# The RWKV stage of a decoder step: from one stream of head pairs with fillers to seven streams that hand over in DRAM

## The chip, the cores and the metric

The kernel runs on one core of a Trainium2 chip. Its time is the device time of one execution in microseconds; lower is better. The core has TensorE (matrix products, into eight PSUM banks), VectorE (DVE), ScalarE (ACT), GpSimd (POOL) and SyncE (SP, which here only issues DMAs). Each engine works through its own instructions in order and waits on semaphores for the others. A wait therefore also holds up whatever stands behind the waiting instruction on the same engine, and that goes for the DMAs in a queue too.

## The reference

One layer of a hybrid decoder is computed for 1024 prompt tokens and for eight sample sequences of eight tokens, 1088 columns in all, with a model width of 1024 and everything in fp32. The part that the change concerns is the RWKV-7 branch (8 heads of 64 channels) and what stands next to it:

```python
P = h @ w_in                                  # RWKV columns | pooling columns | gate columns
xl = pr + (pr_prev - pr) * mu_shift           # token shift
r, k, v, xw, xa, xg = split(xl)
decay = exp(-exp(-softplus(-(w0 + tanh(xw) @ w2)) - 0.5));  a = sigmoid(a0 + xa @ a2)
kk = normalize(k * k_k);  k = k * (1 + (a - 1) * k_a)
# per token and head, S is the 64x64 state:
sa = S @ (-kk);  S = S * decay + outer(sa, kk * a) + outer(v, k);  y = S @ r
y = group_norm(y) * ln_w + ln_b + sum(r * k * r_k) * v;  y = y * (sigmoid(xg) @ g2)
# branch B: causal means over 2, 4, 8, 16 tokens, minus the token, times pool_w
merged = sigmoid(gate_A) * (A @ w_br_rwkv) + sigmoid(gate_B) * (B @ w_br_pool)
x = x + gt * (merged @ w_out)                 # then a squared-ReLU MLP of width 4096, and norms
```

The recurrence over tokens is computed in chunks of 64 tokens: within a chunk its effect is a product with the inverse of a unit triangular 64x64 matrix, and only a 64x64 state goes from chunk to chunk. The prompt has 16 chunks; the 64 sample columns are one more, the 17th, in which eight 8x8 blocks are independent.

## The kernel before

Features lie on the 128 partitions, tokens along the free dimension. Two heads fill the partitions, so that the RWKV work comes in four blocks `f` of two heads.

**Weight jobs.** The large products are jobs in `stream` (line 177). A job takes weights of 128 outputs, splits weights and activations into a high and a low part of the fast fp32r type, and adds three products (`mm3`, line 169) for each of three column chunks `CH` (364, 362, 362 columns). The high part is made on ScalarE (line 165), the low one on GpSimd or VectorE (line 166). A job accumulates in three of four PSUM banks with the tag "mm"; its `consume` moves them out chunk by chunk.

**The order on TensorE is written out by the program.** `Pace.run` (line 87) keeps a clock of its own, to which every matmul adds a planned time. It takes the weight jobs as a background and a list of generators as foreground streams. A stream yields a due time (or a condition); as soon as the clock has reached it, its next step goes in ahead of the next piece of background. The order is fixed from then on: if a step's operands come later than planned, TensorE waits for them, with all that stands behind. The streams use two PSUM banks with the tag "w" and two with the tag "wc". The order on the other engines, SP included, is made by a scheduler.

**Stage 1** (`phase1`, line 1075) runs 34 jobs on `w_in`: 14 blocks of RWKV columns (`rwkv_cols`), 4 of pooling columns (`pool_cols`), 16 of gates (`gate`). Each collects its 1088 columns in a row (`px`, two buffers), finishes them (token shift, running sums, tanh) and stores them in DRAM (`d_x`, `d_th`). Then come eight jobs of the pooling branch (`op_job`), whose results stay in on-chip rows. The foreground streams are `chains`, `heads`, `pools` and `or_rows`. In `heads`, block after block:

- `front(f)`: decay, normalised key and rate over all 1088 columns; it makes `bk` (two operands of the score products, line 562 on VectorE and 563 on GpSimd) and leaves the rest for `unit`;
- `scores(f)`: `unit` for the two halves of the prompt and the sample chunk. It makes `ra` (lines 608 and 609), the score matmuls, masks (lines 628, 629) and transposes;
- `inverse(f)`: the triangular 16x16 blocks by a recursion of 15 steps on VectorE (lines 698, 700). Its tiles have two layers: the 16 prompt chunks, and the sample chunk with 15 empty places;
- `level` and `affine`: from 16x16 to 64x64 on TensorE, and the products that turn a chunk into one affine step;
- beside them, as a filler that `both` interleaves: `sample(f-1)` next to the front, `post(f-1)` (norm, bonus, output gate) next to the inverse.

`chains` (line 1025) carries the state through the 16 chunks: a product, an addition on VectorE (line 831), the next product, planned 2300 ns apart.

**Stage 2** (`phase2`, line 1158) begins with eight jobs of the RWKV branch (`or_job`, line 1176). Each loads a gate row into a tile "t" (four buffers), multiplies it with the product, adds the pooling result on GpSimd (line 1186), and splits the sum (lines 1189, 1190). The modulation weights (`ada`) take tiles of the same tag, two at a time. Then come `w_out`, the MLP and the final norm.

## Time and profile before

| | |
|---|---|
| median of 3 runs | 1866.54 us (1862.32 to 1871.72) |
| the profiled execution: time, span | 1863.12 us, 1861.3 us |
| mean granted TensorE clock | 0.963 |
| RWKV stage, from the first weight job to the last pooling-branch job | 84 to 858 us |
| branch, output and feed-forward jobs | 858 to 1861 us |

The profile shows one execution. Its page gives busy times of each engine, the same in 40 slices, the chain of work that ended last, and the costliest groups of instructions; other views give the waits of an engine, stretches of time, and single instructions. PE is TensorE, PEld its weight loads, PEclk the clock that it was granted, in parts of full speed. A row of the waits names who waited, for whom, the microseconds in all, the number of waits and the longest.

### The profile page before, as it was taken

The numbers are of one execution on the slowest core, as the hardware profiler recorded it, in microseconds if no ns is written. First come the engines' busy times: TensorE is split into PE (matmuls) and PEld (weight loads), VectorE is DVE, ScalarE is ACT, GpSimd is POOL, SyncE is SP. The second block draws the span as 40 slices with busy tenths as digits, with TensorE's granted clock in tenths as the row PEclk, the third lists the DMA queues.
The fourth block names the chain that finished last, engine by engine and source line by source line (L and its number), as shares of the span: only waits on it lengthen the run. The fifth ranks groups of instructions, "written<-read, shape, count | busy, mean of one in ns | idle before, by whom it ended". The sixth has DMA issues, their size and how long they took to land. (4 is left out here: it accounts for less than half of the span.)

```text
span 1861.3 us, 32532 instructions
## 1 busy us (share of the span) xinstructions
PE 1720.2 (92%) x13721; PEld 1597.2 (86%) x13721; DVE 867.1 (47%) x1446; ACT 557.6 (30%) x1085; POOL 421.9 (23%) x444
## 2 busy tenths in 40 slices
PE   3979997999798979998999789999999999999997
PEld 1869786887687779887889789999999999999987
DVE  5365647653765356444423653333333243433335
ACT  4533343343334324321223332222212121212132
POOL 2553234221312132011411431111111111111110
PEclk9989998999898989999999889999999999999999
DMA  8223322332232232445851211111111111111112
GB/s 313 68 85 117 123 68 78 119 99 77 81 114 99 74 107 81 167 142 205 286 184 66 74 57 41 46 46 46 43 44 46 46 46 46 40 46 46 46 46 97
DMA packets 76449, 169.96 MB, mean 91 GB/s; under 512 B 15152, under 2 KB 21808, under 8 KB 76304
## 3 DMA queue, kind: packets, MB, share of 16 engines
q1 hardware_dynamic: 70688, 151.68, 23.9%
q10 hardware_dynamic: 5472, 15.70, 2.5%
q8 instruction: 108, 1.77, 0.4%
q0 software_dynamic: 144, 0.51, 0.1%
q14 instruction: 37, 0.30, 0.1%
HBM read 133.47 MB, written 34.39 MB: 90 GB/s over the span
## 5 line engine op out<-in xcount | busy, mean ns | idle before, releaser
L147 PE MATMUL mm<-hx,whi 128*128 128x362 f32 (+1 forms) x2560 | 680.7, 348 | 9.9 <-DMA hx<-d_orl 3.8
L147 PEld LDWEIGHTS mm<-hx,whi 128*128 128x128 f32 x2560 | 456.8, 193 | 54.4 <-issue 23.1
L166 POOL TENSOR_TENSOR wlo<-wraw,whi 128x512 fp32r<-128x512 f32 x154 | 206.6, 1342 | 1047.0 <-ACT whi L165 1031.7
L147 PE MATMUL mm<-hx,wlo 128*128 128x362 f32 (+1 forms) x1280 | 425.0, 332 | 0.0
L147 PE MATMUL mm<-ma,whi 128*128 128x364 f32 (+1 forms) x1280 | 317.7, 329 | 0.0
L165 ACT ACTIVATE whi<-wraw 128x512 fp32r<-128x512 f32 x240 | 151.2, 630 | 526.7 <-PE w L147 397.5
L147 PEld LDWEIGHTS mm<-hx,wlo 128*128 128x128 f32 x1280 | 247.9, 194 | 0.0
L147 PEld LDWEIGHTS mm<-ma,whi 128*128 128x128 f32 x1280 | 226.0, 189 | 5.1 <-issue 4.3
L147 PE MATMUL mm<-ma,wlo 128*128 128x364 f32 (+1 forms) x640 | 210.2, 328 | 0.0
L1342 DVE SCALAR_TENSOR_TENSOR hx<-mm,aq,hx 128x364 f32<-128x364 f32 (+4 forms) x136 | 75.0, 587 | 214.6 <-PE mm L147 214.4
L147 PE MATMUL w<-mb,whi 128*128 128x362 f32 x640 | 164.0, 337 | 6.0 <-DVE mb L1237 2.1
L147 PEld LDWEIGHTS w<-mb,whi 128*128 128x128 f32 x640 | 117.1, 195 | 8.3 <-DVE mb L1237 2.6
L147 PEld LDWEIGHTS mm<-ma,wlo 128*128 128x128 f32 x640 | 120.6, 188 | 0.0
L166 DVE TENSOR_TENSOR wlo<-wraw,whi 128x512 fp32r<-128x512 f32 x86 | 61.2, 712 | 126.9 <-ACT whi L165 126.9
L1255 DVE TENSOR_TENSOR ft<-ft 128x362 f32<-128x362 f32 (+1 forms) x96 | 51.7, 562 | 137.4 <-ACT ft L1254 137.1
L147 PE MATMUL w<-mb,wlo 128*128 128x362 f32 x320 | 107.7, 337 | 7.2 <-DVE wlo L166 5.9
L147 PE MATMUL w<-hx,whi 128*128 128x362 f32 x416 | 103.5, 330 | 0.0
L1347 POOL TENSOR_TENSOR hx<-hx,rs 128x64 f32<-128x64 f32 x72 | 37.0, 515 | 187.0 <-DVE rs L1345 186.9
L147 PEld LDWEIGHTS w<-hx,whi 128*128 128x128 f32 x416 | 73.7, 191 | 0.9 <-issue 0.9
L303 DVE RECIPROCAL wt<-wt 128x182 f32<-128x182 f32 (+1 forms) x48 | 57.8, 1251 | 29.1 <-ACT wt L301 29.1
L147 PEld LDWEIGHTS w<-mb,wlo 128*128 128x128 f32 x320 | 62.8, 196 | 8.8 <-DVE wlo L166 7.1
L1254 ACT ACTIVATE ft<-mm 128x364 f32<-128x364 f32 x64 | 29.3, 474 | 134.5 <-PE mm L147 134.4
(294 smaller groups left out, 2335.4 us busy)
## 6 DMA issues: line engine op xcount, KB each, us to landing
wraw<-in_w_ff SPq DMA_DIRECT2D x132, 256.0 KB, 2.6
wraw<-in_w_in SPq DMA_DIRECT2D x68, 256.0 KB, 2.8
t<-in_w_ada_mlp SPq DMA_DIRECT2D x24, 512.0 KB, 5.8
wt<-d_x SPq DMA_DIRECT2D x20, 544.0 KB, 3.8
d_th<-px SPq DMA_DIRECT2D x16, 544.0 KB, 2.8
aw<-in_w_ada_mix SPq DMA_DIRECT2D x16, 512.0 KB, 9.9
wraw<-in_w_out SPq DMA_DIRECT2D x32, 256.0 KB, 2.6
d_x<-d SPq DMA_DIRECT2D x14, 512.0 KB, 2.7
```

The source lines that it names most:

```text
L147: return self.nc.tensor.matmul(out, lhsT, rhs, **kw)
L165: nc.scalar.activation(hi, raw, AF.Copy)
L166: (nc.gpsimd if n % 2 or n < self.solo else nc.vector).tensor_tensor(lo, raw, hi.bitcast(F32), op=ALU.subtract)
L303: nc.vector.reciprocal(out[:, a:min(a + 182, n)], out[:, a:min(a + 182, n)])
L1254: nc.scalar.activation(t[:, :n], ps[:, :n], AF.Relu)
L1255: nc.vector.tensor_tensor(t[:, :n], t[:, :n], t[:, :n], op=ALU.mult)
L1342: nc.vector.scalar_tensor_tensor(x[:, c0:c0 + m], ps[:, :m], gt[:, 0:1], x[:, c0:c0 + m], op0=ALU.mult, op1=ALU.add)
L1347: nc.gpsimd.tensor_tensor(x[:, NPR:NT], x[:, NPR:NT], t, op=ALU.add)
```

## The change

- **Token shift by chunks.** `rwkv_cols` no longer collects a row. A chunk is moved out of PSUM twice by ScalarE, scaled by mu and by 1 - mu; VectorE adds the two, one column apart; each chunk is stored by itself. `gate` and `pool_cols` work by chunks too, and the running sums of the pooling branch move from the job into the stream `pools`.
- **Front by pieces.** `front` works on four pieces of four prompt chunks (256 columns; the last with the sample's 64) and stores `bk` and `ra` in DRAM (`d_bk`, `d_ra`). The projections w2 and a2 are padded with zeros to 128 rows.
- **Streams.** `heads` and `both` go. In order of priority there are `chains`, `pairs` (`operands`, `scores`, `rows`, `inverse`, `level`, `affine`), `samples`, `fronts`, `posts`, `pools`, `or_rows`. `operands` loads `bk` and `ra` of half a block; for the next block it is asked for ahead of `level`.
- **A pause.** After a step that used both "w" banks, no other stream but the first and the last goes on for 800 ns of the planner's clock; after a step that used one, 800 ns from the use before.
- **Sample on its own.** `inverse` has one layer. `sample` inverts its 8x8 blocks as (I+X)(I+X^2)(I+X^4), with twelve small products.
- **Norm by pieces.** `post` works on the four pieces, each when its half of the chain is done; the third group of modulation weights is loaded in 16 steps where it had 4.
- **Pooling branch through DRAM.** `op_job` stores its results; `or_job` loads them into a second "t" tile. The rows of the RWKV branch can come as soon as the pooling rows are loaded. A weight job of pooling group g waits until group g-1 is finished.

```diff
@@ Pace.run
-                if r() if callable(r) else r <= self.t:
+                if (self.t >= self.hold or i in free) and (r() if callable(r) else r <= self.t):
+                    self.banks = 0
...
+                    if self.banks:
+                        self.hold = (self.t if self.banks > 1 else self.last) + 800
+                        self.last = self.t
@@ rwkv_cols, consume
+                nc.scalar.activation(p[:, 1:1 + m], ps[:, :m], AF.Copy, scale=mu)
+                nc.scalar.activation(d[:, :n], ps[:, :n], AF.Copy, scale=mu1)
...
+                nc.vector.tensor_tensor(d[:, :m], d[:, :m], p[:, :m], op=ALU.add)
...
+                nc.sync.dma_start(dst[:, c0:c0 + n], d[:, :n])
@@ front, one piece
+            wa, k = load(12, c0, n), load(4 + f, c0, n)
...
+            yield 6500
...
+            self.mm(ps[:, :n], w2a2[:, 0, :], wa, start=True, stop=True)
...
+            yield 1000
             ps = self.ps("w")
+            self.mm(ps[:, :n], self.kc("bones"), sq, start=True, stop=True)
+            self.rinv(ps, n, sq, 1.0, 1)
...
+            nc.sync.dma_start(self.d_bk[f][:, cs], bk[:, :C].rearrange("p c s j -> p (c s j)"))
+            r = load(f, c0, n)
...
+            nc.sync.dma_start(self.d_ra[f][:, cs], ra[:, :C].rearrange("p c s j -> p (c s j)"))
+            nc.vector.scalar_tensor_tensor(r, r, self.par("r_k", f), k, op0=ALU.mult, op1=ALU.mult)
+            v = load(8 + f, c0, n)
...
+            q, v = yield from first(i, c0, n)
+            yield FY
             ps = self.ps("w")
+            self.mm(ps[:, :n], self.kc("bones"), q, start=True, stop=True)
@@ pairs
+            yield from self.scores(f, d, 0)
+            yield from self.operands(f, d, 1)
+            yield from self.rows(f, d, 0)
+            yield from self.scores(f, d, 1)
+            yield from self.rows(f, d, 1)
+            yield from self.inverse(d)
+            if f < 3:
+                yield from self.operands(f + 1, D[f + 1], 0)
+            yield from self.level(d)
+            yield from self.affine(f, d)
@@ inverse, the recursion
-            nc.vector.tensor_tensor(pr, at[:, :, t, 0:t].unsqueeze(2).to_broadcast([P, 2, t, t]),
-                                    tt[:, :, 0:t, 0:t].rearrange("p b i j -> p b j i"), op=ALU.mult)
+            nc.vector.tensor_tensor(pr, at[:, t, 0:t].unsqueeze(1).to_broadcast([P, t, t]),
+                                    tt[:, 0:t, 0:t].rearrange("p i j -> p j i"), op=ALU.mult)
@@ phase1
-        self.pace.run(back, [self.chains(), self.heads(), self.pools(), self.or_rows()])
+        self.pace.run(back, [self.chains(), self.pairs(), self.samples(), self.fronts(), self.posts(), self.pools(), self.or_rows()], free=(0, 6))
@@ or_job
-                t = S["t"] = T()
+                t, S["u"] = T(), T()
+                S["t"] = t
                 nc.scalar.dma_start(t, self.d_th[m])
+                nc.scalar.dma_start(S["u"], self.d_th[8 + m])
...
-                nc.gpsimd.tensor_tensor(t, t, self.tp[m], op=ALU.add)
+                nc.gpsimd.tensor_tensor(t, t, S["u"], op=ALU.add)
@@ constants
-LS = (2300, 2300, 2300, 1500)
+LS = 2000
+FB = 7
+FY = 8000
+UY = (11000, 3500, 3500)
+PC4 = [(0, 256), (256, 256), (512, 256), (768, 320)]
```

## The prediction

> **What bounds the kernel now.** I read the page first: the busy times, the slices and the chain that ended last.

> ```profile
> span 1861.3 us, 32532 instructions
> PE 1720.2 (92%) x13721; PEld 1597.2 (86%) x13721; DVE 867.1 (47%) x1446; ACT 557.6 (30%) x1085; POOL 421.9 (23%) x444
> ...
> PE   3979997999798979998999789999999999999997
> ...
> PEclk9989998999898989999999889999999999999999
> ...
> PE 42%; DVE 3%; ACT 0%; issue 0%; POOL 0%; DMA 0%; DVEq 0%; POOLq 0%; ACTq 0%
> ```

> TensorE is the bound: 92% busy, and the chain is made of its work. What can be won is its idle time, its time at a lower clock, and work taken from it. I then cut the span into the stages of the code: the RWKV stage from its first weight job to the last branch-pool job (84 to 858), the passage to the second stage (858 to 872), the branch jobs and what follows (872 to 985), and the long feed-forward part. The columns are busy time and count of each engine, granted clock, share of the DMA engines, GB/s.

> ```profile
> 84.00:858.00 774.00, 705.04 (x7688) 617.47 (x7687) 428.33 (x673) 275.73 (x578) 194.61 (x196) 0.95 0.31 103
> 858.00:872.00 14.00, 6.78 (x28) 5.05 (x27) 3.47 (x6) 0.63 (x1) 1.73 (x2) 0.83 0.99 387
> 872.00:985.00 113.00, 108.72 (x646) 93.31 (x645) 43.05 (x79) 28.47 (x45) 32.59 (x17) 0.98 0.61 214
> 1090.00:1780.00 690.00, 690.00 (x4159) 690.00 (x4159) 246.29 (x461) 151.69 (x296) 103.65 (x115) 1.00 0.14 45
> ```

> The feed-forward part has nothing to give. The RWKV stage has 774 - 705 = 69 us without TensorE work, the passage 7.2 us. The waits of TensorE between 84 and 858 say for what:

> ```profile
> PE w L147 <- POOL ra L609: 39.0, 4, 11.0
> PE w L147 <- DVE hv L729: 5.4, 3, 2.1
> ...
> PE w L147 <- ACT iv L634: 2.8, 4, 1.4
> PE w L147 <- ACT wt L521: 2.7, 3, 1.4
> ```

> Four waits, one for each block of two heads, make 39.0 of the 69 us: the first scores of a block stand in TensorE's order before their operand `ra` has come out of the front (line 609 on GpSimd). Each also costs time after it, seen at the one that ended at 134.54:

> ```profile
> 134.54 2.15 PE L147 MATMUL w<-ra,bk 64*128 64x128 f32 x16 [10.97 <-POOL ra L609]
> ...
> 137.69 0.81 PE L147 MATMUL mm<-hx,whi 128*128 128x362 f32 x2
> 138.29 0.51 PE L147 MATMUL mm<-hx,wlo 128*128 128x362 f32 x1
> 138.59 0.81 PE L147 MATMUL mm<-hx,whi 128*128 128x364 f32 x2
> ...
> 140.38 0.50 PE L147 MATMUL mm<-hx,whi 128*128 128x362 f32 x2
> ...
> 140.88 0.49 PE L147 MATMUL mm<-hx,whi 128*128 128x364 f32 x2
> 141.47 1.16 PE L147 MATMUL w<-ra,bk 64*128 64x128 f32 x16
> ```

> The same sixteen instructions take 2.15 us after the wait and 1.16 once warm, and a triple of weight matmuls 0.90 us (137.69 to 138.59) against 0.50 (140.38 to 140.88). About 1.0 on the scores and four triples at 0.3 to 0.4 give 2.3 us for each wait, 9.2 for the four.

> **The change part by part.** Sums go against the profiled execution: 1863.1 us around a span of 1861.3; the median of the three runs, 1866.5, lies 3.4 above it.

> ```profile
> wt<-d_x SPq DMA_DIRECT2D x20, 544.0 KB, 3.8
> ```

> *Scores no longer wait for the front: -48.2.* Fronts run as a stream of their own, a quarter at a time, and hand `bk` and `ra` over in DRAM; a block's operands are asked for one whole block earlier, behind `inverse`. What is late next is their load: 512 KB twice, behind a store; the nearest row is a load of 544 KB on the same queue, 3.8 us to landing. Only the second half of a block's operands is asked for a few steps ahead of use; that is hidden by `rows` of the first half, whose due times alone are 6.1 us. I take all of 39.0 + 9.2, and as the low end 30, if a quarter of it comes back as waits for these loads.

> *TensorE gets more work: +14.* These rows are of the RWKV stage:

> ```profile
> L147 PE MATMUL w<-at,z 64*64 64x64 f32 x256 | 16.1, 223 | 0.0
> ...
> L147 PE MATMUL w<-wt,sw 64*128 64x362 f32 x32 | 7.5, 516 | 0.0
> L147 PE MATMUL w<-wt,sw 128*128 128x362 f32 x16 | 6.3, 472 | 0.0
> L147 PE MATMUL w<-wt,sw 64*128 64x364 f32 x16 | 3.5, 518 | 0.0
> L147 PE MATMUL w<-wt,sw 128*128 128x364 f32 x8 | 3.2, 481 | 0.0
> ```

> The decay and rate projections go from 64 rows (7.5 + 3.5 = 11.0 us) to a zero-padded 128 rows. The output gate has that shape on half the columns for 9.5, so they become 19.0: +8. The squared inverse of the sample adds twelve 64x64 products a block; 256 instructions are 128 products in 16.1 us, 0.126 each: 48 x 0.126 = +6. Nothing hides TensorE's own work. Ends: +8 (work put into gaps) and +20 (changes of shape between them).

> *The recursion of `inverse` loses its second layer: -3.* On VectorE all its products, reductions and transposes are halved. VectorE is no bound (428 of 774 us); what the stage gains is what waits for it, the 5.4 us at line 729 in part. Ends 0 and -8 (with the 2.8 at line 634).

> *A pause of 800 ns after a step that used both "w" banks: -4.* It lets weight matmuls run where TensorE now waits for a bank (the 2.7 at line 521 and others of its kind). Ends 0 and -10. The price is slower streams, hidden as long as weight jobs are left, which they are: by the due times in the code the streams need an estimated 565 us (80 to the first operands; four blocks of 58 us of due times in `pairs` and some 47 of own work, pauses and other streams' steps; 65 for the last chain and norm), against some 700 us of TensorE work.

> *Token shift on ScalarE: +5.* Each of the 14 column jobs now reads a bank twice, with scale mu and 1 - mu:

> ```profile
> L388 ACT ACTIVATE px<-mm 128x362 f32<-128x362 f32 x12 | 5.7, 471 | 0.4 <-PE mm L147 0.2
> ...
> L390 ACT ACTIVATE px<-mm 128x64 f32<-128x64 f32 x12 | 2.7, 225 | 0.0
> ...
> L301 ACT ACT_TABLE_LOAD x8 | 10.3, 1283 | 4.8 <-DVE hv L903 4.2 <-DVE hx L1154 0.4
> ```

> A chunk holds its bank for about 0.47 more, and 0.2 for its halo (a short copy takes 0.225). Four banks serve jobs of three chunks, a chunk is done every 0.5 us, so the second chunk of the next job can come 0.3 to 0.5 us early: 14 x 0.35 = 5. Ends 0 (a stream's step lies between) and 20 (ScalarE busy elsewhere, table loads included). On VectorE the same part takes work away; nothing waits there.

> *The front as sixteen pieces: +8.* After the norm matmul of a piece, its bonus matmul is due 8000 ns later; in between lie a square root, the reciprocals, seven VectorE operations and three of GpSimd. Today's chain for 1088 columns at block 0:

> ```profile
> 109.09 1.28 ACT L301 ACT_TABLE_LOAD   x1
> 110.39 0.56 ACT L301 ACTIVATE wt<-w,eps 128x364 f32<-128x364 f32 x1
> ...
> 118.00:135.70 17.70, 6.73 (x44) 6.43 (x44) 17.47 (x14) 1.11 (x2) 11.64 (x7) 0.74 0.30 97
> ...
> 118.13 2.42 DVE L303 RECIPROCAL wt<-wt 128x182 f32<-128x182 f32 x2
> ...
> 132.38 2.10 POOL L609 TENSOR_TENSOR ra<-wt,e 128x512 f32<-128x512 f32 x1
> 133.49 2.15 DVE L568 SCALAR_TENSOR_TENSOR wt<-wt,part,wt 128x1088 f32<-128x1088 f32 x1
> ```

> From 118.13 VectorE works on it for 17.5 us, and two earlier pairs of reciprocals add 4.84; a quarter is 5.6. With a table load 1.28, the root 0.4, `ra` on GpSimd half of 2.10 and the matmul and handovers some 0.5, the piece needs 8.8 us against 8.0, so 16 x 0.8 = 13 if each step falls on its due time; chains and pairs go first and push many of them back: I take 8. Ends: 0, and 56 at 3.5 us each, if other streams' work stands between on VectorE, whose share grows from 55% to some 65% while the streams last.

> [...]

> *The passage: -3.* Rows of branch A are loaded while the pool jobs run, into tiles that the pool results no longer hold, so the 7.2 us go; eight loads of pool rows now have no stream beside them, where I put +4 for an idle stretch of the kind in the passage. Ends -7 and +10.

> *Branch jobs with two tiles each: +18.* Each of the eight jobs now takes two of the four "t" tiles (gate and pool half), and the modulation weights hold the other two, so the tiles of job m+1 are those of job m. Today:

> ```profile
> t<-d_th ACTq DMA_DIRECT2D x8, 544.0 KB, 5.4
> ...
> 877.98 2.53 POOL L1186 TENSOR_TENSOR t<-t,hx 128x1088 f32<-128x1088 f32 x1 [16.89 <-DVE t L1182]
> ...
> 931.28 2.54 POOL L1186 TENSOR_TENSOR t<-t,hx 128x1088 f32<-128x1088 f32 x1
> ...
> 880.55 0.81 ACT L1189 ACTIVATE ma<-t 128x726 fp32r<-128x726 f32 x1 [4.70 <-POOL t L1186]
> 881.26 0.49 ACT L1189 ACTIVATE mb<-t 128x362 fp32r<-128x362 f32 x1
> ```

> The first and last of eight adds are 53.3 us apart, 7.6 a job. After: add 2.5, the split some 2.3 (0.81, 0.49 and VectorE behind), then the second load may go, 5.4 to landing, and the next add: 10.2. Seven times 2.6 is 18. Ends 6 (landing in 3.8) and 34 (the split 2.2 later, behind other VectorE work). Out-projection needs all eight results, so nothing hides it.

> Sum: -48.2 + 14 - 3 - 4 + 5 + 8 - 3 + 18 = -13; 1863.1 - 13 = 1850.

> **The rivals.** *The streams mesh:* fronts and branch loads stay hidden, bank waits go: -48.2 + 14 - 8 - 10 + 0 + 0 - 7 + 6 = -53, so 1810. For it: VectorE and ScalarE are half idle. Against: the tile count in the branch jobs.
> *The front takes the place of its own wait (slower):* TensorE waits at the bonus matmul of every piece, as it does at the scores today. The row for it is the planner's miss there: 11 us late where 6.5 and a little were planned. At 3.5 us a piece the term is 56 instead of 8: 1898. It decides (0.5% slower than the median) from 2.1 us a piece. Against: short pieces.
> *Nothing left:* the branch jobs at 34 take what is over: 1850 + 16 = 1866.

> **How the numbers follow.** Half a per cent, 9.3 us, is about what a measurement of this kernel tells from no change. The forecast has 0.36 (its own range 1830 to 1857, faster), the streams meshing 0.15, nothing left 0.13, the front's wait 0.36. Faster 0.51, same 0.13, slower 0.36. The range goes from the meshing case, with a little below, to the front's wait and a little above: 1800 to 1908.

> **What would show it.** No wait at the scores for GpSimd, and no half-speed matmuls after them; a granted clock over 0.95 in the RWKV stage; waits at the bonus matmul (`q`, or its bank) counted by sixteen; adds of the branch jobs 10 us apart; the streams done well before the weight jobs. Wrong it is if TensorE waits at new places of the streams, above all for loads behind the one SyncE queue, which gets some three times as many DMAs, or if the streams outlast the weight jobs.

## The result and the profile after

The changed kernel takes 1962.79 us (median of 4 runs, 1961.89 to 1966.78). The kernel before, run beside it, takes 1869.01 us (4 runs, 1862.32 to 1871.72). The ratio is 1.0511, 95% interval 1.0477 to 1.0546: the change makes the kernel 5% slower, where 1850 us and a gain were predicted, and the range ended at 1908.

The page of the profiled execution: its span, the busy times, TensorE's row of the slices and the clock's, and the chain that ended last.

```profile
span 1961.3 us, 34317 instructions
...
PE 1769.8 (90%) x13905; PEld 1636.1 (83%) x13905; DVE 842.2 (43%) x1617; ACT 660.5 (34%) x1333; POOL 406.0 (21%) x487
...
PE   3798899878869889899789988999999999999997
...
PEclk8899989989979889999999988999999999999998
...
PE 40%; DVE 3%; ACT 1%; issue 0%; DMA 0%; POOL 0%; DVEq 0%; POOLq 0%; ACTq 0%
```

TensorE is still the bound, and it lost in two ways at once. Its busy time grew by 49.6 us (1720.2 to 1769.8), and the time in which it did nothing by 50.4 (span less busy time, 141.1 to 191.5). Together that is the whole difference of the two spans, 100.0 us.

The trace also records the granted clock: every record of it is 1.0 or 0.5 of full speed, 40 records before and 60 after. Stretches at half speed hold 91.8 us of TensorE's busy time before and 142.5 after. An estimate takes half of that as lost: then 25 of the 49.6 us are half speed and 24 are added work. The same sum, busy time less half of what falls into such stretches, gives 1674 to 1675 us for the kernel before and its two variants below, and 1696 to 1702 for the kernel after and the eleven runs below that keep its work on TensorE. So the added work is nearly the same in all of them, and what else differs in busy time is the clock.

The same cut as in the prediction shows the place: the RWKV stage, the passage, and the branch jobs with what follows.

```profile
84.00:949.80 865.80, 764.97 (x7953) 668.74 (x7952) 409.22 (x852) 384.11 (x839) 184.53 (x251) 0.93 0.41 128
949.80:964.00 14.20, 7.02 (x43) 6.61 (x44) 0.69 (x1) 0.63 (x1) 1.80 (x2) 0.87 1.03 411
964.00:1090.00 126.00, 115.39 (x660) 96.76 (x656) 44.97 (x82) 28.40 (x45) 32.73 (x17) 0.95 0.58 199
```

The RWKV stage took 774 us and takes 865.8. Of these 92 us, 60 are busy time of TensorE (705 to 765) and 32 idle time (69 to 101). The passage is as long as it was (14.2 against 14.0), and all that follows takes 8 us more (from the end of the passage to the end of the span, 989.3 before and 997.3 after).

Now TensorE's waits of that stretch, with the start of the modulation weights in it (52 to 960 us). The columns are as in the prediction: who waited for whom, microseconds in all, number of waits, the longest.

```profile
PE w L152 <- DMA g<-d_y: 25.9, 8, 5.0
PE w L152 <- ACT iv L646: 11.6, 17, 2.6
PE wc L152 <- DMA g<-in_w_ada_mix: 10.2, 1, 10.2
PE w L152 <- ACT f L310: 7.6, 6, 2.6
PE w L152 <- DVE f L595: 7.3, 2, 5.5
PE w L152 <- ACT uv L685: 6.9, 5, 4.3
...
PE mm L152 <- ACT wp L401: 3.1, 4, 2.2
```

The four waits for `ra`, 39.0 us, are gone, as predicted. In their place stand many others. The largest row is for the load of the chain's result `d_y` by the norm pieces of `post`, eight times 1.0 to 5.0 us. Added up by engine, the waits for ScalarE are more: 49 us in 47 waits between 84 and 949.8 us, where the kernel before has 11 us in 14. The bonus matmul of the front (`f` L595), which one rival made the new bound, waits only twice.

### The profile page after: what moved, and what is told of

Same layout as the page of the kernel before. It is cut to its first block, busy times and chain, and to the rows that moved or that the text cites. A ratio compares the mean times of both kernels' runs of the same rounds, so it can differ in the third digit from the quotient of the medians.

```text
span 1961.3 us, 34317 instructions
## 1 busy us (share of the span) xinstructions
PE 1769.8 (90%) x13905; PEld 1636.1 (83%) x13905; DVE 842.2 (43%) x1617; ACT 660.5 (34%) x1333; POOL 406.0 (21%) x487
## 3 DMA queue, kind: packets, MB, share of 16 engines
q1 hardware_dynamic: 115104, 179.55, 28.3%
## 5 line engine op out<-in xcount | busy, mean ns | idle before, releaser
L152 PEld LDWEIGHTS mm<-hx,whi 128*128 128x128 f32 x2560 | 462.2, 195 | 47.3 <-issue 19.2
L152 PE MATMUL w<-hx,wlo 128*128 128x362 f32 x208 | 67.8, 326 | 0.0
## 6 DMA issues: line engine op xcount, KB each, us to landing
t<-d_th ACTq DMA_DIRECT2D x16, 544.0 KB, 5.2
```

The source lines that it names most:

```text
L152: return self.nc.tensor.matmul(out, lhsT, rhs, **kw)
```

## The experiments

Three theories stood at the start. **A:** the written due times are too short for what now stands behind them (a load from DRAM, a move by ScalarE), TensorE waits, and after each wait it works at half speed for a while. **B:** the change gives TensorE more work than I counted. **C:** the streams have become so long that they outlast the weight jobs. A time is quoted with its ratio to the kernel before, run on the same chip, and the interval of the ratio. Differences between runs are between medians; they were made on several chips, and the ratios give the same within 6 us.

### All due times of the streams times 1.4

```diff
-                        live[i] = r if callable(r) else self.t + r
+                        live[i] = r if callable(r) else self.t + r * 1.4
```

> All due times of the RWKV stage's streams are 1.4 times as long; no work is changed. Theory A (steps stand in TensorE's order before their operands are there, since the due times are too short for seven streams at once, and half-speed matmuls follow each wait): of the 97 us of waits between 60 and 870 us some 60 go and a third of the half-speed time with them, 1962 becomes 1880 to 1905. Rival B (the loss is added TensorE work and the low clock of its many small products, whatever the order): no better than 1945. Rival C (the streams already set the length of the stage): slower than 1962.

Measured: 1931.38 us (1.0353, 1.0334 to 1.0373), a gain of 31 and between the ranges of all three theories. The stage is shorter by 56 us (809.4 against 865.8), but the next stretch gives much of it back. First the stage and the stretch behind it, then TensorE's waits from 890 to 960:

```profile
84.00:893.40 809.40, 738.60 (x7928) 648.83 (x7927) 407.61 (x839) 374.04 (x829) 184.87 (x250) 0.96 0.42 133
893.40:950.00 56.60, 30.68 (x132) 24.04 (x131) 15.81 (x27) 7.69 (x16) 8.04 (x5) 0.73 0.68 251
```

```profile
PE mm L153 <- DMA hx<-d_orh: 10.7, 1, 10.7
PE w L153 <- DMA g<-d_y: 7.9, 1, 7.9
```

Both A and C hold in part. Longer due times take away waits and half speed (TensorE's busy time in the stage falls by 26 us with nearly the same work); 1.4 is too much, since the last norm then ends behind the weight jobs, and the rows of the RWKV branch (`d_orh`) are late.

### The norm pieces and the modulation weights

The first edit moves two due times: the norm pieces' load from 7500 to 14000 ns ahead of use, and the third group of modulation weights 25 us later.

```diff
@@ post
-            yield 7500
+            yield 14000
@@ posts
+        yield 25000
         yield from self.ada_fill()
```

> Only two due times change: the norm pieces wait 14 us for their loads where they waited 7.5, and the modulation weights start 25 us later. Theory A: the waits for d_y (25.9 us) and for the modulation weights (10.2) go, with 5 to 10 us of half speed behind them: 1962 becomes 1917 to 1930, and the other waits stay. Rival B: the waits move to other steps of the same streams, 1950 to 1962.

Measured: 1922.31 us (1.0307, 1.0289 to 1.0326), 40 us less. No wait for `d_y` and none for `in_w_ada_mix` is left. Later, each edit ran alone.

> Of the two edits that together gave 40 us, only the norm pieces' due time, 7500 to 14000 ns. If the waits for d_y and the slow matmuls behind them are the larger part: 1925 to 1940 us. If the early modulation weights were: 1948 to 1958 us.

> Of the two edits that together gave 40 us, only the modulation weights' start 25 us later. The wait of 10.2 us at the first weight step and some 3 us behind it go: 1945 to 1953 us. Above 1958 us would say that the wait only moves to the next operand that the start of the stage lacks.

The norm pieces' due time alone: 1936.29 us (1.0383, 1.0354 to 1.0412), 27 less than the changed kernel. The modulation weights alone: 1962.86 us (1.0526, 1.0491 to 1.0560), nothing. The 10.2 us wait goes there, but TensorE is no sooner done; the row "waits for `d_y`" is 27.2 us in that run.

### Why the load of `d_y` was late

A longer due time cures it but doesn't say what was late. A norm piece loads three tiles of a ring `g` and uses a fourth; the ring has five buffers. Two runs changed one thing each. The first gave the chain result's tile a free buffer (four for the loaded tiles, one for the fourth tile), the second also sent the two stores that end a piece from ScalarE's queue.

```diff
-            y, bv, sg, sq = (self.piece("g", 5)[:, :n] for _ in range(4))
+            y, bv, sg = (self.piece("g", 4)[:, :n] for _ in range(3))
+            sq = self.piece("gs", 1)[:, :n]
...
-            nc.sync.dma_start(self.d_or[0][f][:, s], sq)
+            nc.scalar.dma_start(self.d_or[0][f][:, s], sq)
```

> The norm pieces take three tiles of the ring g (now four buffers, the fourth tile of a piece has a buffer of its own), so that the chain result of the next piece has a free buffer at once; the due time of 7500 ns is kept. Theory R (the load of d_y is issued late because its buffer is the one whose store ends the piece before): the 25.9 us of waits for d_y fall below 10, and with the slow matmuls behind them the kernel gains 15 to 35 us: 1928 to 1948 us. Rival T (7500 ns are too few for the store of the chain result and the load that follows it, whatever the buffers): more than 18 us of these waits stay, and the kernel is at 1955 us or above.

> As the run with the ring of four and one, and the two stores that end a norm piece go out from ScalarE's queue in place of SyncE's. Theory Q (the load of the next chain result stands in SyncE's queue behind these two stores, which wait for the whole VectorE and ScalarE chain of the piece; neither buffers nor the due time of 7500 ns are to blame): the waits for d_y fall from 26 us below 8, and 20 to 40 us of the time go: 1922 to 1942 us. Rival T (the loads are late with any queue): more than 18 us of the waits stay, 1955 us or above. A fall of the waits without a gain would say that the weight jobs behind them were late anyway.

Measured: 1962.25 us (1.0505, 1.0483 to 1.0526) and 1973.64 us (1.0575, 1.0549 to 1.0601). The waits for `d_y` were 26.2 and 24.2 us, so both simple answers fell. SyncE's own waits say more. These rows are of the kernel after (the first two) and of the run with the other queue (the last two), from 300 to 860 us:

```profile
SPq L167 <- POOL wlo L171: 50.2, 21, 8.7
...
SPq L955 <- DVE g L971: 31.6, 7, 7.6
```

```profile
SPq L956 <- DMA d_orl<-g: 30.2, 10, 5.1
SPq L956 <- DVE g L972: 28.3, 6, 6.4
```

The loads of a piece stand one behind another in SyncE's queue. One that waits until VectorE has read its buffer for the last time (31.6 us in 7 waits), or until a store has left it (30.2 us in 10 waits with the other queue), holds up `d_y` behind it, whichever buffer `d_y` has. The queue also stands for others, 50.2 us for weight loads whose buffer GpSimd still reads (the first row). The example, SyncE and then TensorE in the kernel after:

```profile
490.97 0.37 SPq L843 DMA_DIRECT2D d_y<-y  x1
...
533.84 0.32 SPq L617 DMA_DIRECT2D bk<-d_bk  x1
534.26 0.44 SPq L955 DMA_DIRECT2D g<-d_bv  x1
...
535.27 0.37 SPq L976 DMA_DIRECT2D d_orl<-g  x1
535.70 0.46 SPq L955 DMA_DIRECT2D g<-d_y  x1
```

```profile
536.72 0.59 PE L152 MATMUL w<-g,sw 128*128 128x256 f32 x2
542.31 1.19 PE L152 MATMUL w<-g,kct 128*128 128x256 f32 x2 [4.99 <-DMA g<-d_y]
542.94 1.17 PE L152 MATMUL mm<-hx,whi 128*128 128x364 f32 x2
```

This is the sixth of sixteen such loads, and the sixth of sixteen such stores is the one at 491.0: the chain had sent its result to DRAM 45 us before the load was issued. So the store of the chain was not what came late. The load was issued at 535.7, behind the end of the piece before and a load of 512 KB, and TensorE stood until 542.3. Behind it the matmuls run at half speed, 1.17 us for a pair that takes about 0.5 warm. The last run of this line gave the loaded tiles six buffers, two full sets, with stores on SyncE's queue and the due time of 7500 ns as before; the room came from the sample's mask product, which takes a shared tile.

```diff
-            y, bv, sg, sq = (self.piece("g", 5)[:, :n] for _ in range(4))
+            y, bv, sg = (self.piece("g", 6)[:, :n] for _ in range(3))
+            sq = self.piece("gs", 1)[:, :n]
@@ sample
-        s0, um = (self.p1.tile(...) for t in ("s0", "um"))
+        s0 = self.p1.tile(...)
...
+            um = self.hv()
```

> Six buffers for the three loaded tiles of a norm piece and one for the fourth (the room comes from the sample's mask product, which takes a shared tile), stores on SyncE's queue and the due time of 7500 ns as in the kernel after. In SyncE's waits of the kernel after the load of d_bv stands for VectorE's last read of the piece before (31.6 us in 7 waits), and the load of d_y behind it. Theory RQ (ring and queue together: the load that waits for a buffer holds up the one that could go): with two full sets of buffers that wait goes, the waits of TensorE for d_y fall from 26 below 8, and 20 to 40 us of the time go: 1922 to 1942 us. Rival T (7500 ns don't cover the store of the chain result and the load in any order): above 1952 us.

Measured: 1933.09 us (1.0373, 1.0344 to 1.0402), 30 us less, with no wait of TensorE for `d_y` in the list. SyncE's issues in that run:

```profile
489.39 0.32 SPq L958 DMA_DIRECT2D g<-d_y  x1
...
492.60 0.38 SPq L958 DMA_DIRECT2D g<-d_y  x1
```

The second piece's `d_y` goes out at 492.6, right behind the first piece's, where it went at 535.7. In the four blocks this second load follows its store by 2.8 to 5.3 us, in the kernel after by 18 to 48. SyncE still waits 55 us for weight loads in this run, so those alone were not the cause; with the buffers the waits for `d_y` are gone. The rival that 7500 ns are too few in any order falls with that. That a load without a buffer holds up those behind it in the queue is read from SyncE's waits; no run sends the loads themselves out from another queue. In the run with the stores on ScalarE's queue, which was 11 us slower than the changed kernel, the loads still stand for buffers (28.3 and 30.2 us in the rows above), and that is cause enough for its waits for `d_y`.

### The work of TensorE

> The decay and rate projections use 64 rows again, as before the change. By the rows before (11.0 us) and after (16.5 + 5.4 us) the added work is 11 us. Rival B (added work counts in full): 1951. Theory A (work added beside waits is partly covered by them): 1955 to 1962.

```diff
-            self.mm(ps[:, :n], w2a2[:, 0, :], wa, start=True, stop=True)
+            self.mm(ps[:, :n], w2a2[0:64, 0, :], wa[0:64], start=True, stop=True)
```

(and the same for the second projection). Measured: 1981.63 us (1.0621, 1.0595 to 1.0648), 19 us slower than the changed kernel, which neither theory had expected. The group itself became cheaper (18.4 against 21.9 us), but each change of planned time moves all later steps against each other, and in the profiled run idle time grew by 4 us and busy time by 8. The estimate of its work at full speed, 1703 us, is 4 above the changed kernel's, where it should be lower. Why the kernel lost as much as 19 us is left open. So this small edit couldn't be priced by its time on a kernel with so many waits. The groups of the trace still show where TensorE's time went. First four groups of the kernel before, then those that answer to them after (the line, shapes and count, then busy us and mean ns, then the idle time before them; the norm products of front and `post` were one group before and are four now):

```profile
L147 PE MATMUL w<-wt,kct 128*128 128x362 f32 x64 | 27.1, 512 | 9.8 <-DVE hv L729 5.4 <-DVE wt L936 3.8 <-ACT wt L301 0.5
...
L147 PE MATMUL w<-wt,kct 128*128 128x364 f32 x32 | 12.9, 485 | 2.3 <-ACT wt L548 2.3
...
L147 PE MATMUL wc<-wt,sT 128*9 128x512 f32 x32 | 4.4, 623 | 0.0
...
L147 PE MATMUL w<-hv,ab 128*64 128x512 f32 x16 | 4.3, 618 | 0.0
```

```profile
L152 PE MATMUL w<-g,kct 128*128 128x256 f32 x48 | 18.1, 464 | 24.6 <-DMA g<-d_y 23.2 <-ACT f L310 0.8 <-DVE wp L513 0.6
L152 PE MATMUL w<-f,kct 128*128 128x256 f32 x48 | 17.1, 440 | 19.5 <-DVE f L595 7.3 <-ACT uv L685 4.3 <-DVE at L671 4.3
...
L152 PE MATMUL w<-f,w2a 128*128 128x256 f32 x48 | 16.5, 450 | 2.7 <-ACT uv L685 1.3 <-ACT iv L646 0.7 <-DVE zx L919 0.2
...
L152 PE MATMUL wc<-g,sT 128*9 128x256 f32 x64 | 10.8, 396 | 10.2 <-DMA g<-in_w_ada_mix 10.2
...
L152 PE MATMUL w<-um,ab 128*64 128x512 f32 x16 | 9.5, 676 | 1.1 <-ACT iv L646 1.0
...
L152 PE MATMUL w<-g,kct 128*128 128x320 f32 x16 | 7.4, 547 | 7.3 <-ACT uv L785 4.1 <-DMA g<-d_y 2.6 <-ACT f L310 0.5
...
L152 PE MATMUL w<-f,kct 128*128 128x320 f32 x16 | 6.0, 455 | 2.3 <-ACT z L746 2.3
...
L152 PE MATMUL w<-f,w2a 128*128 128x320 f32 x16 | 5.4, 450 | 0.4 <-ACT z L746 0.3
```

Norm products 40.0 to 48.6, projections 11.0 to 21.9, modulation weights 4.4 to 10.8, the sample's last product 4.3 to 9.5: 31 us more in these four, where I had counted the projections' 8 alone. Some of it is time at half speed: in the combination of the next section, with fewer waits, the same four groups take 45.8, 19.2, 9.7 and 8.6 us, 24 more than before.

### Due times, row tile and work together

The combination: due times times 1.2, norm pieces at 14000, modulation weights later, and the pool half of a branch job in a row of its own in place of a second "t" tile. That last edit also ran alone.

```diff
@@ or_job
-                t, S["u"] = T(), T()
+                t, S["u"] = T(), HX(F32)
```

> The pooling half of a branch job is loaded into a row of its own (eight of them, in the rows that the pooling operands leave) instead of the second tile of four. The prediction's term (tiles of job m+1 are those of job m): adds 7 to 8 us apart instead of 9, 1962 becomes 1950 to 1955. Rival (the branch jobs are late for another reason, such as the 7.2 us wait for modulation weights at the passage): 1960 to 1964, spacing unchanged.

> The kernel after with due times of the RWKV streams times 1.2, the norm pieces' 7500 at 14000 (times 1.2 too), the modulation weights begun 25 us later, and the pool half of the branch jobs in a row of its own. Theory A (waits from due times that are too short make most of the loss, extra work of TensorE the rest): the gains add, 40 for the norm pieces and weights, 12 for the branch jobs, 10 to 20 for the rest: 1890 to 1905 us, still above the kernel before. Rival S (longer due times only move the waits to the end, as the streams then outlast the weight jobs): 1915 us or above. Under 1875 would say that extra work costs nothing.

The tile alone: 1950.93 us (1.0476, 1.0455 to 1.0497), 12 us less by the medians and 6.5 by the ratios, whose intervals overlap. The first and last add on GpSimd of the kernel after, then of that run:

```profile
967.76 2.53 POOL L1196 TENSOR_TENSOR t<-t,t 128x1088 f32<-128x1088 f32 x1 [12.42 <-DVE t L1192]
...
1030.93 2.53 POOL L1196 TENSOR_TENSOR t<-t,t 128x1088 f32<-128x1088 f32 x1 [0.29 <-DMA t<-d_th]
```

```profile
956.24 2.52 POOL L1196 TENSOR_TENSOR t<-t,hx 128x1088 f32<-128x1088 f32 x1 [11.55 <-DVE t L1192]
...
1008.66 2.54 POOL L1196 TENSOR_TENSOR t<-t,hx 128x1088 f32<-128x1088 f32 x1
```

Adds are 9.0 us apart with two tiles of the shared ring (63.2 us for seven) and 7.5 with the row, as before the change (7.6). The profiled run of this kernel also has a shorter stage 1, whose code is the same: it is the fastest of its five and had a granted clock of 0.962, the others 0.950 to 0.954. So only the 10.7 us between the adds are shown to be the tile's.

The combination: 1903.10 us (1.0186, 1.0169 to 1.0203), within what was expected by adding the gains. Its busy times:

```profile
PE 1751.9 (92%) x13905; PEld 1623.3 (85%) x13905; DVE 845.7 (44%) x1617; ACT 659.0 (35%) x1333; POOL 408.4 (21%) x487
```

Its span is 1902.2, so TensorE is idle for 150.3 us, 9 more than in the kernel before (141.1), and busy for 31.7 more. Stretches at half speed hold 110.1 us of its busy time, 91.8 before; by the estimate above 9 of the 31.7 us are half speed and 23 are work. So work is the larger part of what the combination still loses to the kernel before: theory B, with 23 us where 14 were counted. The last run of this line takes back two pieces of that work, the 64 rows and the sample's last product in one step for both halves.

```diff
@@ sample
-        for h, hs in enumerate(HB):
-            nc.vector.tensor_tensor(qv(um), ...)
-            yield 3500
-            ps = self.ps("w")
-            self.mm(ps[hs, :], ab[:, h, 64:128], um, start=True, stop=True)
+        ums = [um, self.hv()]
+        ...
+        yield 4500
+        ps = self.ps("w")
+        for h, hs in enumerate(HB):
+            self.mm(ps[hs, :], ab[:, h, 64:128], ums[h], start=True, stop=True)
```

> The combination of longer due times (1903 us), with two pieces of TensorE work taken back: the decay and rate projections on 64 rows again, and both halves of the sample's last product in one step, so that they run side by side. By the busy rows of the traces this is 3.5 and 5.2 us. Theory W (TensorE is the bound, so work taken from it comes off the time once the waits are covered): 1890 to 1898 us. Rival J (the step is lost in changes of order elsewhere, as the 64 rows alone were in the kernel after, 19 us slower): 1903 us or above.

Measured: 1895.00 us (1.0168 to the kernel before, 1.0143 to 1.0193), 8.1 less than the combination by the medians and 3 by the ratios, whose intervals overlap; 8.7 were expected by rows. TensorE is busy for 1745.7 us, 6.2 less, and the estimate of its work at full speed is 1691, 5.5 less. So on a plan with few waits the work comes off TensorE's busy time, and some of it off the time; how much is not settled. On the plan with many waits the same 64 rows gained nothing.

### The pause

```diff
-                        self.hold = (self.t if self.banks > 1 else self.last) + 800
+                        self.hold = (self.t if self.banks > 1 else self.last) + 0
```

> The pause of 800 ns between the steps of different streams is taken away. Theory A (the prediction's: it keeps steps from waiting for each other's PSUM banks): without it the waits of TensorE in the RWKV stage grow, by 4 us or more, and many short ones on evictions by ScalarE and VectorE come in: 1967 to 1985 us. Rival P (the pause pushes steps together so that they bunch up behind it, and costs): 1940 to 1957 us. No change would say that the pause does nothing either way.

> The combination of longer due times (1903 us) without the pause of 800 ns. Theory L (the pause saved 49 us in the kernel after because it slows the streams, that is, lengthens due times that are too short; with longer ones it is hardly needed): 1903 to 1918 us. Rival B (it keeps steps of different streams from meeting on the two banks, which longer due times don't do): 1930 to 1955 us.

In the changed kernel: 2011.53 us (1.0771, 1.0748 to 1.0794), 49 us slower without the pause, more than either theory had expected. In the combination: 1915.95 us (1.0271, 1.0248 to 1.0294), 13 slower. The busy row of the first:

```profile
PE 1792.5 (89%) x13905; PEld 1651.0 (82%) x13905; DVE 842.3 (42%) x1617; ACT 657.3 (33%) x1331; POOL 404.1 (20%) x487
```

The same instructions keep TensorE busy for 22.7 us more than with the pause, and its idle time grows by 23.1 (span 2007.1). The 22.7 are the clock: stretches at half speed hold 190.3 us of busy time, with the pause 142.5. Some three quarters of the pause's worth go once due times are long. That fits a pause that works mainly as a lengthening of due times that are too short; what the last quarter is was not tried.

### The kernel before with one number changed

```diff
@@ before, unit
-        yield 6500 if u == 0 else 3000 if u == 1 else 2000
+        yield 17500 if u == 0 else 3000 if u == 1 else 2000
```

> The kernel before, with one number changed: the first scores of a block are due 17500 ns after the front's end where it was 6500. Theory D (the four waits for ra were a miss of the planner, and a longer due time alone takes them away while weight jobs cover it): the 39.0 us of waits and most of the 9 us behind them go: 1815 to 1840 us, faster than both kernels. Rival H (the one serial stream of heads is what sets the end of the stage, so that 4 x 11 us later only move the wait to where the weight jobs have run out): 1858 to 1880 us.

> The kernel before with the scores due at 17500 ns, and now the change's pause of 800 ns as well, between the steps of its one stream of heads; against the run with 17500 alone, 1842 us. Theory M (the pause pays only where several streams put steps one behind another; with one stream the next step stands at its own due time anyway): 1838 to 1852 us. Rival P (each pair of steps that shares the two banks gains, as in the kernel after): 1805 to 1832 us. Rival E (the stream gets longer than the weight jobs): above 1860 us.

Measured: 1842.31 us (0.9861, 0.9840 to 0.9882), 1.4% faster than the kernel before, just above the range that was expected, and the fastest of all. With the pause as well: 1845.28 us (0.9888, 0.9863 to 0.9914), no difference to tell. The busy row and the main waits of the run with 17500:

```profile
PE 1720.2 (94%) x13721; PEld 1594.6 (87%) x13721; DVE 868.5 (47%) x1446; ACT 559.1 (30%) x1085; POOL 421.1 (23%) x444
```

```profile
PE wc L147 <- DVE S L831: 10.9, 8, 3.6
...
PE w L147 <- POOL ra L609: 5.5, 1, 5.5
```

The waits for `ra` fell from 39.0 to 5.5 us, but the time by 24.6: waits in the chain (`S`, 0.7 before, 10.9 now) and others took part of the place, and TensorE's busy time is the same to a tenth of a microsecond, with 92.9 us of it at half speed where there were 91.8, so nothing came from warmer matmuls.

## Why the prediction was wrong

**What bounds the kernel, and which waits go.** Right. TensorE bounds both kernels, the four waits for `ra` are gone, and no matmul of the scores waits for GpSimd.

**"Scores no longer wait for the front: -48.2."** The mechanism was right, the size too large. What these waits are worth is shown on the kernel before only: with the longer due time 33.5 of the 39.0 us go, and the time falls by 24.6 us, less even than the low end of 30. I took each wait as a sum that is paid back in full. In an order written out ahead, TensorE then comes earlier to the next operand, which can be late in its turn, as the chain's was (0.7 to 10.9 us). The 9.2 us for half speed did not come at all.

**The step that failed: that nothing else in the streams waits.** The sum had terms for the scores, the bonus matmul and the passage, but none for `post` and none for the new moves of short pieces. The largest single loss of idle time, 25.9 us of waits for `d_y` with slow matmuls behind five of the eight (1.19 us for the pair of 128x256 products that takes 0.67 behind two of the others), was in a step of the change that I had described and not priced, the norm by pieces. With buffers for it the kernel gains 30 us, with a longer due time 27. My last sentence named it (loads behind the one SyncE queue), as a thing that would make the prediction wrong, but without a term and a chance. The many short waits for ScalarE's moves and roots (`iv` 11.6, `f` L310 7.6, `uv` 6.9; in all 49 us where there were 11) had no term beyond the token shift's either. Nor had the half speed behind the new waits, some 25 us: I had named a granted clock over 0.95 in the stage as a sign, and it fell from 0.95 to 0.93.

**"TensorE gets more work: +14."** The two parts that I counted came out as predicted or nearly: the twelve squares 6.9 us (+6 predicted), the projections +10.9 (+8). For the projections that is partly luck: with 64 rows again they still take 18.4 us where they took 11.0 uncut, so the padding that I had priced is 3.5 of the 10.9, and the rest is pieces and half speed. The others were missed: norm products +8.6, modulation weights +6.4, the sample's last product +5.2. I had counted added products and not the same products cut into smaller ones. In all the added work is about 24 us by the estimate above, over my end of 20.

**"A pause: -4."** Mis-sized by far in the kernel as it is: 49 us. But most of it goes where due times are longer: on the combination it gives 13, on the kernel before with its longer due time nothing.

**"The front as sixteen pieces: +8"**, with the rival that made it 56. The bonus matmul waited 7.3 us in two waits, the longest 5.5, so the rival's mechanism, on which I had put 0.36, did not happen. That 7.3 lies near my 8 is luck: I had added up sixteen misses of 0.8. The kernel ended slower for another reason than the one that I gave for that side. A table load takes 1.28 us, as I had counted, and in 47 of the 55 between 84 and 949.8 us ScalarE's next operation starts within 0.04 us of the load's end. What I had overlooked is their number, 55 where there were 15. The norm pieces take a root as the front's pieces do, and the row of these roots has 27 of them:

```profile
L310 ACT ACT_TABLE_LOAD x27 | 34.6, 1283 | 3.3 <-DMA wp<-d_th 1.7 <-DVE tt L708 0.7 <-DMA d_th<-gp 0.5
```

Forty more loads are 51 of the 108 us by which ScalarE's busy time grew in the stage. About 8 of the 49 us in which TensorE waited for ScalarE fall on them directly; no run takes them away.

**"Branch jobs with two tiles each: +18."** Mechanism right, as the run with a row in place of the second tile shows; size too large: 1.4 us a job in place of 2.6, 10 us in all, inside the ends of 6 and 34.

**Token shift +5, passage -3.** Four waits for `wp` make 3.1 us. The passage is as long as it was: the loads that I saw going went, and a wait of 7.2 us for a modulation weight took their place. The recursion's single layer (-3) was not tried alone.

**"Slower streams are hidden as long as weight jobs are left."** True up to a point that I had not placed: at 1.2 the combination keeps its gain, at 1.4 the stage ends on the last norm.

These parts don't add up to 94 us one by one, since each moves the order of all others; what adds up is the pair from the profiles, 50 us of idle time and 50 of busy time. Of these, the combination takes back 41 and 18. By the estimate above the 50 us of busy time are about half clock and half work. Open remains how the waits for ScalarE divide between its table loads, its other work and due times, and why the 64 rows alone cost 19 us.

## What to carry to other kernels

In a plan that fixes TensorE's order ahead, price each step's due time against what now stands behind it, for all steps that the change touches and not only for those that wait today; a wait that goes is worth its length only if the next operand is in time (here 24.6 of 33.5 us). Before a rebuild, try the one number: a longer due time gave 1.4% at once. And count loads by buffers: with all loads in one queue, a ring with less than two full sets held up even the load whose buffer was free (25.9 us of waits for `d_y` with five buffers, none listed with two full sets).

## What the runs showed of the hardware

**Two products for different halves of the result ran side by side where they stood next to each other.** The sample's last product, as in the run that takes work back, and in the kernel after:

```profile
266.45 0.64 PE L153 MATMUL w<-um,ab 128*64 128x512 f32 x1
266.46 0.64 PE L153 MATMUL w<-hv,ab 128*64 128x512 f32 x1
```

```profile
268.75 1.07 PE L152 MATMUL w<-um,ab 128*64 128x512 f32 x2
...
273.36 1.07 PE L152 MATMUL w<-um,ab 128*64 128x512 f32 x2
```

In one step both start within 0.01 us, and the two halves take 1.08 us together (to 267.53); in two steps they take 1.07 us each.
